# Five small edits to a one-core hybrid decoder layer: turned roots by way of DRAM, block ends shared by VectorE and GpSimd, fill and stores moved

## The chip, the core and the metric

The kernel runs on one core of one Trainium2 chip. The metric is the device time of one execution in microseconds (us). The engines are TensorE (PE, its weight loads PEld), VectorE (DVE), ScalarE (ACT), GpSimd (POOL) and SyncE (SP), which only issues DMAs.

## What is computed

One decoder layer over 1024 tokens of width 1024, in float32. A root-mean-square norm feeds one wide input projection. Mixer A is sparse attention (8 heads in 2 groups, blocks of 128 queries, three branches: compressed, selected, window); mixer B is gated linear attention in chunks. Both are projected up, gated, summed and projected out; a SwiGLU channel mixer and a last norm follow. Cut to what matters:

```python
h = rmsnorm(x, norm_mix)
q_nsa, kv_nsa, g_nsa, q_gla, k_gla, v_gla, lr_gla, r_gla, g_merge = split(h @ w_in)
o_a = nsa_attention(...)            # per 128 queries: gt0 * o_c + gt1 * o_s + gt2 * o_w
o_b = rmsnorm(gla_chunked(...), gla_norm) * silu(r_gla)
merged = gate_a * (o_a @ w_up_nsa) + gate_b * (o_b @ w_up_gla)
x = x + merged @ w_out
h = rmsnorm(x, norm_ffn)
x = x + (silu(h @ w_ffn_gate) * (h @ w_ffn_up)) @ w_ffn_down
return rmsnorm(x, norm_final)
```

## The kernel before, in words

Every large product is made of three TensorE products of split operands: each float32 operand is a high part (rounded by ScalarE, L356, L1150, L1252) and the rest (a subtraction on VectorE or GpSimd, L357, L1151, L1253), and high x high, high x rest and rest x high are summed in PSUM. Activations stand transposed, features on the partitions and tokens along the row, so one matmul is 128x128 weights on 512 tokens.

TensorE's order is written by hand (`manual_schedule` for PE). The order on VectorE, ScalarE, GpSimd and SyncE is made by the tile framework's scheduler, which simulates time, except for instructions in `keep_in_program_order`; the helper `load` (L496) issues a DMA on SyncE in that way.

**Fill.** Work that TensorE can do at any time stands in a queue of small items (`Fill`, L72): a group is three matmuls, planned at 648 ns. `fill.run(ns)` emits groups until their planned time is used up, `flush` emits what is left. So the total of the fill is the same however it is spread.

**First stage (to about 115 us).** The first projection runs as the inputs land; then `work`, a list of groups with other items between them, is flushed in order (L738). `first_roots` (L571) multiplies the sums of squares by ones on TensorE (L573, L574), computes the root `rbc` of each token on ScalarE and VectorE, spread over all partitions, and scales six results. It stands behind 2 of the 16 groups of the first job. `root_turned` (L579) stands behind all 16: eight tiny products with a 1x1 one (L582, 16 instructions, since float32 takes two each) turn row 0 of `rbc` into `rtok`, 128 tokens a column, and VectorE copies it out. `rtok` scales the token-major projections (`token_proj`, L721), first by ScalarE at L756.

**Gated linear attention (about 189 to 300 us).** `gla_stream` (L909) walks 8 chunks: `gla_diag` (L845), seven levels (`gla_level`, L853), and, after level 2, the operands of the next chunk (`gla_prep`, L796: exponents on GpSimd L821 and ScalarE, products `xq` on VectorE L828 and `xx` on GpSimd L832). Each `yield` gives a planned time, and `fill.run(cost * ratio)` puts that share of four projection jobs behind it; `ratio` (L955) is the fill's cost over the sum of the yields. A level writes one of three PSUM banks, which VectorE reads (L861).

**Attention (about 365 to 790 us).** 16 units (two groups of 8 query blocks) of five branches. `Plan` (L109) is a planner with costs and free times of the engines, which decides in what order TensorE gets scores, transposes (L1173, L1157), products with the values (L1182, L1165) and fill. The output of a unit stands in the one PSUM bank `o`; when its last branch is in, `finish` (L1188) empties it: ScalarE copies the lower half of the partitions to the upper (`fo`, L1195), then VectorE adds the two halves in two instructions into `oa` (L1197), and only then may the next unit's first product (L1165) write `o`. The planner knows it as 478 ns of ScalarE followed by 670 ns of VectorE (L214 to L217). `unit` (L1025) prepares the next queries: a load of `rp`, VectorE shuffles, three GpSimd instructions (L1033 to L1035), four DMAs, a ScalarE copy and a GpSimd subtraction (L1044, L1045). Behind the planner's end, `oa` of both groups is split into `oah` and `oal` by ScalarE and VectorE (L1252, L1253), in the middle of what is left of the attention.

**The rest.** Merge and output projection (to about 947 us), then the channel mixer in a form with seven instead of eight block products, 11 pairs of weight blocks up and 11 down. At the end the last products are made in two parts of the tokens, 320 and 192 wide (`finish_half`, L1712): VectorE adds the part to the residual (`plus`, L1588), ScalarE squares (L1593), TensorE sums (L1682), ScalarE and VectorE make the root (L1684 to L1688), and VectorE scales each of eight blocks (`store`, L1602), which SyncE or ScalarE's queue then sends out. `when(i, ...)` puts a step in front of group i.

Of the kernel before, what the change touches and what calls it, by code (L numbers as in the profile page):

```python
# [100 lines left out]
LAT, WAIT, LOADED, COPIED = 155.0, 300.0, 1500.0, 3000.0  # L101
NBIG, NMID, NSMALL = 18, 10, 8
SCRATCH = 2048
FINE, NGATE = 3, 2

UP = (1, 2, 4, 5, 7)

# [1 line left out]
class Plan:  # L109
# [100 lines left out]
    def value(self):  # L210
        _, later, n, b, last = self.pend.popleft()
        later()
        self.t += 218.0 * n if b.br else 436.0
        if last and b.br == 2 and b.j == 1:  # L214
            t = self.on("A", self.t, 478.0)
            t = self.on("D", t, 670.0)
            self.o = t + LAT  # L217

    def run(self):
        ops = dict(T=(self.turn_at, self.turn), S=(self.score_at, self.score), P=(self.value_at, self.value))  # L220
# [21 lines left out]
def layer_kernel(ctx, tc, a, outT):  # L242
# [36 lines left out]
    def ps_o():  # L279
        return bank("o")  # L280
# [30 lines left out]
    def hs(hf):  # L311
        return slice(512 * hf, 512 * (hf + 1))

    def bs(b):
        return slice(128 * b, 128 * (b + 1))
# [255 lines left out]
    def first_roots():  # L571
# [4 lines left out]
        for n in (2, 3, 4, 5, 0, 1):  # L576
            scaled(dst[n], acc[n] if n > 1 else dst[n], n % 2, 0.125 if n < 4 else None)

    def root_turned():  # L579
        ps = ps_o()  # L580
        for b in range(NB):
            PE.matmul(ps[:, b:b + 1], rbc[0:1, bs(b)], ones[0:1, 0:1], start=True, stop=True)  # L582
        V.tensor_copy(rtok, ps[:, :NB])

    def proj(evac, bank=ps_m, fine=False):

# [134 lines left out]
    def token_proj(parts, ncol, evac, after={}):  # L721
        for b in range(NB):
# [6 lines left out]
            for fn in after.get(b, []):  # L729
# [3 lines left out]
    j1, h1, t1, s1 = compress_job(1)  # L733
    lb, wb = token_weights(a["w_b"], 512, 2)
    work = dense([(a["w_t"][3], proj(lambda p, hf: scaled(kg[hf][:, 1, :], p, hf))), j0, key_job(0), j1, key_job(1)], ready=first)
    fill.add(work[:5] + [(900.0, first_roots), (0.0, load_consts)] + work[5:20] + [(400.0, root_turned)] + work[20:48] + h0 + work[48:59] + t0
             + work[59:63] + s0 + work[63:69] + lb[:1] + work[69:74] + lb[1:2] + work[74:84] + h1 + lb[2:] + work[84:])
    fill.flush()  # L738

# [169 lines left out]
    def gla_stream():  # L909
        for c in range(NB):  # L910
            gla_diag(c)
            yield 860
            for i in range(NLV):
                gla_level(c, i)
                yield 430
                if i == 1 and c:
                    gla_out(c - 1)
                    yield 1710
                if i == 1 and c < NB - 1:
                    gla_turn(c)  # L920
                    yield 220
                if i == 2 and c + 1 < NB:
                    gla_prep(c + 1)
                    yield 430
                if i == 3 and c in (1, 3):
                    turn_rank(c // 2 + 2)
                    yield 430
                if i == 4 and c < NB - 1:
                    gla_state(c)
                    yield 860  # L930
                if i == 5 and c in (1, 3):
                    decay(c // 2 + 2)
                    yield 860
        yield 500
        gla_out(NB - 1)
        yield 1710
# [15 lines left out]
        return a["w_t"][8 + 2 * g + j], proj(lambda p, hf: scaled(qr[g][hf][:, j, :], p, hf, 0.125))  # L952

    fill.add(dense([query_job(0, 0), query_job(0, 1)] + [gate_job(j) for j in range(NGATE)]))
    ratio = fill.cost() / (8 * (860 + 7 * 430 + 3220) + 1500)  # L955
    for cost in gla_stream():
        fill.run(cost * ratio)
    fill.flush()
# [89 lines left out]
    class Branch:  # L1048
# [139 lines left out]
        def finish(self):  # L1188
            g, i = self.g, self.i
            po = UN[g, i]["o"]  # L1190
            hf = i // 4
            if oa[g][hf] is None:
                oa[g][hf] = big("oa", shape=(2, 512))
            fo = mid("fo")
            S.activation(fo[0:64, :], po[64:128, :], AF.Copy)  # L1195
            for par in range(2):
                V.tensor_add(oa[g][hf][64 * par:64 * par + 64, :, bs(i % 4)],  # L1197
                             po[0:64, :].rearrange("p (j r q) -> p j r q", j=2, r=2)[:, :, par, :],
                             fo[0:64, :].rearrange("p (j r q) -> p j r q", j=2, r=2)[:, :, par, :])
            del UN[g, i]  # L1200


# [45 lines left out]
    for g in range(NG):  # L1248
        for j in range(2):
            th, tl = big("oah", F32R), big("oal", F32R)  # L1250
            for hf in range(2):
                S.activation(th[:, hs(hf)], oa[g][hf][:, j, :], AF.Copy)  # L1252
                V.tensor_tensor(tl[:, hs(hf)], oa[g][hf][:, j, :], f(th[:, hs(hf)]), OP.subtract)  # L1253
            oah.append(th)
            oal.append(tl)
    fill.flush()
# [339 lines left out]
        else:  # L1596
            sums[n].append(sq)

    def store(blk, mp, hf, c=slice(0, 512)):
        m = mp + (MH if blk[0] == "2" else 0)  # L1600
        xv, at = x1[blk, mp][:, c], slice(512 * hf + c.start, 512 * hf + c.stop)
        V.scalar_tensor_tensor(xv, xv, gains[:, 2, m:m + 1], rbc[:, at], op0=OP.mult, op1=OP.mult)  # L1602
        (S if c.start and mp % 2 else SP).dma_start(outT[:, m, at], xv)


# [85 lines left out]
    ALL = 4  # L1691
# [20 lines left out]
    def finish_half(i, h):  # L1712

        for mp in range(MH):
            when(i + mp // 2, plus, "21", mp, ps["A"][mp], H[h])
            when(i + mp // 2, square, "21", mp, 0, False, H[h])
        when(i + 2, roots, 0, H[h])
        when(i + 2, sums[0].__delitem__, slice(1, None))
        for k in range(2 * MH):
            when(i + 5 + k // 2, store, "12"[k // MH] + "1", k % MH, 0, H[h])  # L1720

    with tc.manual_schedule(engines={mybir.EngineType.SP}):
        for i in range(3):
# [105 lines left out]
```

## Time and profile before

| what | value |
|---|---|
| median of 3 runs | 1596.46 us (1591.89 to 1596.6) |
| the profiled execution, its own time | 1600.53 us |
| its span, first to last instruction | 1598.7 us |
| granted TensorE clock, mean | 0.998 |
| TensorE busy | 1567.5 us, 98% |
| VectorE, ScalarE, GpSimd busy | 1010.4, 814.4, 678.3 us |

The page shares the span out: busy time, forty slices, queues, the chain of work that ended last, the costliest groups. A wait is an engine's idle time before an instruction, with the instruction that ended it. A matmul of 512 columns is shown with 0.39 us, but the next one starts 0.227 us later; stretches of TensorE are therefore read from start to start.

### The profile page before, as it was taken

How to read it: one execution, taken by the hardware profiler on the slowest of the kernel's cores; microseconds unless marked ns; L12 is line 12 of the kernel's file. 1: busy time of each engine (PE TensorE's matmuls, PEld its weight loads, DVE VectorE, ACT ScalarE, POOL GpSimd, SP SyncE). 2: the span in 40 equal slices, each digit the busy share in tenths (PEclk: the TensorE clock that was granted, in tenths of full speed). 3: DMA queues.
4: the chain of work that ended last, by engine and by line, in shares of the span. 5: the costliest groups of instructions: out<-in, count | busy, mean ns of one | idle time of the engine just before them, and what ended most of it. 6: DMA issues, size and time to landing. Idle time of an engine off the chain costs nothing.

```text
span 1598.7 us, 23059 instructions
## 1 busy us (share of the span) xinstructions
PE 1567.5 (98%) x8047; PEld 1311.5 (82%) x8047; DVE 1010.4 (63%) x1653; ACT 814.4 (51%) x1632; POOL 678.3 (42%) x590
## 2 busy tenths in 40 slices
PE   9999999999999999999999999999999999999998
PEld 7888988888888888888877878888888888888887
DVE  7681487586777677677564477744444444499785
ACT  6241555575676676677653344433433444454542
POOL 6110366562212233130144440466666666556570
PEclk9999999999999999999999999999999999999999
DMA  5431112232112122131466532323323323695423
GB/s 182 132 102 61 60 53 68 96 106 83 46 52 65 62 77 65 45 109 60 138 210 206 192 116 73 119 99 106 104 101 105 105 99 99 240 362 162 140 72 125
DMA packets 109590, 179.85 MB, mean 112 GB/s; under 512 B 12689, under 2 KB 29730, under 8 KB 109474
## 3 DMA queue, kind: packets, MB, share of 16 engines
q1 hardware_dynamic: 105442, 171.95, 32.8%
q10 hardware_dynamic: 4032, 6.44, 1.1%
q8 instruction: 63, 1.03, 0.3%
q14 instruction: 53, 0.43, 0.1%
HBM read 128.27 MB, written 45.88 MB: 109 GB/s over the span
## 4 chain that ended last, share of the span: by engine, by line
PE 82%; DVE 6%; DMA 4%; ACT 3%; issue 3%; POOL 2%; SPq 0%; DVEq 0%; POOLq 0%; ACTq 0%
PE m L410 12%; PE d L410 10%; PE m L1397 9%; PE m L1398 9%; PE m L1396 9%; PE m L1759 4%; PE m L1760 4%; PE m L1758 4%; PE o L1182 3%; PE t L1173 3%; PE s L1094 2%; PE s L1095 2%; PE t L725 1%; PE t L726 1%; PE t L727 1%
## 5 line engine op out<-in xcount | busy, mean ns | idle before, releaser
L357 POOL TENSOR_TENSOR wl<-wf,wh 128x512 fp32r<-128x512 f32 x106 | 145.1, 1371 | 323.7 <-ACT wh L356 312.5
L1396 PE MATMUL m<-xt,wh 128*128 128x512 f32 x412 | 160.3, 389 | 0.0
L1397 PE MATMUL m<-xt,wh 128*128 128x512 f32 x412 | 160.3, 389 | 0.0
L1398 PE MATMUL m<-xt,wl 128*128 128x512 f32 x412 | 160.3, 389 | 0.0
L1326 POOL TENSOR_TENSOR wl<-ws,wh 128x512 fp32r<-128x512 f32 x76 | 107.5, 1419 | 73.4 <-ACT wh L1325 73.4
L1151 DVE TENSOR_TENSOR ptl<-t,pth 128x512 fp32r<-128x512 f32 (+1 forms) x168 | 99.4, 596 | 35.5 <-ACT pth L1150 32.5
L1326 POOL TENSOR_TENSOR wl<-wr,wh 128x512 fp32r<-128x512 f32 x69 | 92.2, 1337 | 69.6 <-ACT wh L1325 69.6
L1325 ACT ACTIVATE wh<-ws 128x512 fp32r<-128x512 f32 x76 | 48.0, 632 | 131.4 <-PE m L1397 114.7
L1150 ACT ACTIVATE pth<-t 128x512 fp32r<-128x512 f32 (+1 forms) x168 | 88.0, 525 | 52.8 <-PE t L1173 46.9
L1325 ACT ACTIVATE wh<-wr 128x512 fp32r<-128x512 f32 x87 | 55.0, 632 | 116.9 <-POOL wl L1326 76.4
L1758 PE MATMUL m<-xb,wh 128*128 128x512 f32 x280 | 109.5, 391 | 0.3 <-DVE g L1458 0.3
L1759 PE MATMUL m<-xb,wh 128*128 128x512 f32 x280 | 109.0, 389 | 0.0
L1760 PE MATMUL m<-xb,wl 128*128 128x512 f32 x280 | 108.9, 389 | 0.0
L1326 POOL TENSOR_TENSOR wl<-wd,wh 128x512 fp32r<-128x512 f32 x56 | 82.8, 1482 | 58.3 <-ACT wh L1325 54.7
L410 PE MATMUL m<-hh,wh 128*128 128x512 f32 x240 | 100.4, 419 | 0.0
L1326 DVE TENSOR_TENSOR xb<-ar,xb 128x512 fp32r<-128x512 f32 x73 | 80.3, 1117 | 31.8 <-ACT xb L1325 31.8
L410 PE MATMUL m<-hh,wl 128*128 128x512 f32 x240 | 93.8, 391 | 0.0
L410 PE MATMUL m<-hl,wh 128*128 128x512 f32 x240 | 93.7, 390 | 0.0
L356 ACT ACTIVATE wh<-wf 128x512 fp32r<-128x512 f32 x106 | 65.9, 625 | 53.6 <-PE m L410 25.1
L1396 PEld LDWEIGHTS m<-xt,wh 128*128 128x128 f32 x412 | 77.3, 188 | 16.2
L1398 PEld LDWEIGHTS m<-xt,wl 128*128 128x128 f32 x412 | 77.3, 188 | 16.0
L1397 PEld LDWEIGHTS m<-xt,wh 128*128 128x128 f32 x412 | 77.3, 188 | 16.0
(414 smaller groups left out, 4545.5 us busy)
## 6 DMA issues: line engine op xcount, KB each, us to landing
ar<-actd SPq DMA_DIRECT2D x77, 256.0 KB, 2.8
wf<-in_w_t SPq DMA_DIRECT2D x58, 256.0 KB, 2.9
wr<-in_w_gate SPq DMA_DIRECT2D x44, 256.0 KB, 2.7
wr<-in_w_upf SPq DMA_DIRECT2D x44, 256.0 KB, 2.7
wd<-in_w_down SPq DMA_DIRECT2D x33, 256.0 KB, 5.2
zd<-zt SPq DMA_DIRECT2D x32, 256.0 KB, 2.0
wf<-in_w_out SPq DMA_DIRECT2D x32, 256.0 KB, 3.2
actd<-t SPq DMA_DIRECT2D x30, 256.0 KB, 2.0
```

What stands on the lines that cost most here:

```text
L357: (eng or V).tensor_tensor(wl, wf, f(wh), OP.subtract)
L410: PE.matmul(st["p"], w, x, start=k + i == 0, stop=k == n - 1 and i == 2)
L1150: S.activation(th[:, :c], pt[:, :c], AF.Copy)
L1151: V.tensor_tensor(tl[:, :c], pt[:, :c], f(th[:, :c]), OP.subtract)
L1325: S.activation(th, src, AF.Copy)
L1326: eng.tensor_tensor(tl, src, f(th), OP.subtract)
L1396: PE.matmul(ps, wh[:, c], xh, start=first and k == 0, stop=False, skip_group_check=not first)
L1397: PE.matmul(ps, wh[:, c], xl, start=False, stop=False, skip_group_check=not first)
L1398: PE.matmul(ps, wl[:, c], xh, start=False, stop=k == MH - 1, skip_group_check=not first)
L1758: PE.matmul(dst, wh[:, c], xh, start=first and p == 0, stop=False, skip_group_check=not first)
L1759: PE.matmul(dst, wh[:, c], xl, start=False, stop=False, skip_group_check=not first)
L1760: PE.matmul(dst, wl[:, c], xh, start=False, stop=p == NP - 1, skip_group_check=not first)
```

## The change

Five edits.

1. `root_turned` writes row 0 of `rbc` to DRAM and reads it back with tokens on the partitions, two `load`s on SyncE, in place of eight products and a copy. It needs no place in TensorE's order; its cost in `work` is 0.
2. `first_roots` stands behind 4 groups instead of 2.
3. The yield behind `gla_diag` is 860 + 1200 ns instead of 860, in `ratio` too.
4. `finish`: VectorE copies the upper half out of PSUM (in program order) beside ScalarE's copy, and GpSimd adds; the last unit keeps the old way. The planner counts the longer of 478 (ScalarE) and 550 ns (VectorE). The splits of group 0's `oah` and `oal` go from ScalarE and VectorE to GpSimd.
5. Of the eight blocks of the 320-wide part, the last three are scaled and stored behind the adds of the 192-wide part instead of ahead of them.

```diff
-FINE, NGATE = 3, 2
+FINE, NGATE, AHEAD = 3, 2, 1200
...
         if last and b.br == 2 and b.j == 1:
-            t = self.on("A", self.t, 478.0)
-            t = self.on("D", t, 670.0)
-            self.o = t + LAT
+            self.o = max(self.on("A", self.t, 478.0), self.on("D", self.t, 550.0)) + LAT
...
+    rtd = dr.tile([1, T], F32, name="rtd")
+
     def root_turned():
-        ps = ps_o()
-        for b in range(NB):
-            PE.matmul(ps[:, b:b + 1], rbc[0:1, bs(b)], ones[0:1, 0:1], start=True, stop=True)
-        V.tensor_copy(rtok, ps[:, :NB])
+        load(rtd, rbc[0:1, :])
+        load(rtok, rtd.rearrange("o (b p) -> p (o b)", p=128))
...
-    fill.add(work[:5] + [(900.0, first_roots), (0.0, load_consts)] + work[5:20] + [(400.0, root_turned)] + work[20:48] + h0 + work[48:59] + t0
+    fill.add(work[:7] + [(900.0, first_roots), (0.0, load_consts)] + work[7:20] + [(0.0, root_turned)] + work[20:48] + h0 + work[48:59] + t0
...
             gla_diag(c)
-            yield 860
+            yield 860 + AHEAD
...
-    ratio = fill.cost() / (8 * (860 + 7 * 430 + 3220) + 1500)
+    ratio = fill.cost() / (8 * (860 + AHEAD + 7 * 430 + 3220) + 1500)
...
-            fo = mid("fo")
+            fo, end = mid("fo"), (g, i) == units[-1]
             S.activation(fo[0:64, :], po[64:128, :], AF.Copy)
+            if not end:
+
+                t = mid("fp")
+                tc.keep_in_program_order(V.tensor_copy(t[0:64, :], po[0:64, :]))
+                po = t
             for par in range(2):
-                V.tensor_add(oa[g][hf][64 * par:64 * par + 64, :, bs(i % 4)],
-                             po[0:64, :].rearrange("p (j r q) -> p j r q", j=2, r=2)[:, :, par, :],
-                             fo[0:64, :].rearrange("p (j r q) -> p j r q", j=2, r=2)[:, :, par, :])
+                (V if end else P).tensor_tensor(
+                    oa[g][hf][64 * par:64 * par + 64, :, bs(i % 4)],
+                    po[0:64, :].rearrange("p (j r q) -> p j r q", j=2, r=2)[:, :, par, :],
+                    fo[0:64, :].rearrange("p (j r q) -> p j r q", j=2, r=2)[:, :, par, :], OP.add)
...
             for hf in range(2):
-                S.activation(th[:, hs(hf)], oa[g][hf][:, j, :], AF.Copy)
-                V.tensor_tensor(tl[:, hs(hf)], oa[g][hf][:, j, :], f(th[:, hs(hf)]), OP.subtract)
+                if g:
+                    S.activation(th[:, hs(hf)], oa[g][hf][:, j, :], AF.Copy)
+                else:
+                    P.tensor_copy(th[:, hs(hf)], oa[g][hf][:, j, :])
+                (V if g else P).tensor_tensor(tl[:, hs(hf)], oa[g][hf][:, j, :], f(th[:, hs(hf)]), OP.subtract)
...
-    def store(blk, mp, hf, c=slice(0, 512)):
+    def store(blk, mp, hf, c=slice(0, 512), late=False):
...
-        V.scalar_tensor_tensor(xv, xv, gains[:, 2, m:m + 1], rbc[:, at], op0=OP.mult, op1=OP.mult)
+        ins = V.scalar_tensor_tensor(xv, xv, gains[:, 2, m:m + 1], rbc[:, at], op0=OP.mult, op1=OP.mult)
+        if late:
+            tc.keep_in_program_order(ins)
...
         for k in range(2 * MH):
-            when(i + 5 + k // 2, store, "12"[k // MH] + "1", k % MH, 0, H[h])
+
+            late = h == 0 and k > MH
+            when(i + (NP - ALL + 2 if late else 5 + k // 2), store, "12"[k // MH] + "1", k % MH, 0, H[h], late)
```

## Rows read from the trace of the kernel before

**Rows 1.** The page, busy time (us), share and instructions of each engine.
```profile
PE 1567.5 (98%) x8047; PEld 1311.5 (82%) x8047; DVE 1010.4 (63%) x1653; ACT 814.4 (51%) x1632; POOL 678.3 (42%) x590
```

**Rows 2.** TensorE's waits, 185 to 300 us: total, times, longest (us).
```profile
PE t L859 <- DVE xq L828: 2.3, 4, 0.8
PE t L859 <- DVE at L861: 2.1, 2, 1.6
```

**Rows 3.** TensorE's waits, 365 to 790 us.
```profile
PE t L1173 <- DVE rr L1105: 1.9, 1, 1.9
PE o L1165 <- DVE oa L1197: 1.7, 2, 1.2
PE s L1071 <- ACT p L1125: 1.7, 1, 1.7
PE t L1173 <- DVE ptl L1151: 1.3, 2, 0.7
```

**Rows 4.** Timeline of TensorE, first stage: start us, us, instruction, idle before.
```profile
38.25 0.39 PE L410 MATMUL m<-hh,wh 128*128 128x512 f32 x1
...
39.38 0.39 PE L410 MATMUL m<-hh,wl 128*128 128x512 f32 x1
40.89 0.49 PE L573 MATMUL o<-ssh,onesr 128*128 128x512 f32 x1 [1.12 <-ACT ssh L568]
41.62 0.50 PE L574 MATMUL o<-ssl,onesr 128*128 128x512 f32 x1 [0.23 <-DVE ssl L569]
...
42.55 0.39 PE L410 MATMUL m<-hh,wh 128*128 128x512 f32 x1
...
52.19 1.94 PE L582 MATMUL o<-ones,rbc 1*128 1x1 f32 x16
54.06 0.50 PE L410 MATMUL m<-hh,wh 128*128 128x512 f32 x1
```

**Rows 5.** DMA issues: tiles, queue, count, KB each, median us to landing.
```profile
zd<-zt SPq DMA_DIRECT2D x32, 256.0 KB, 2.0
...
w<-in_cmp_w SPq DMA_DIRECT2D x2, 64.0 KB, 7.1
...
ggain<-in_gla_norm SPq DMA_DIRECT2D x1, 0.5 KB, 3.2
```

**Rows 6.** Timeline of SyncE's queue and of ScalarE, first stage.
```profile
51.54 2.90 SPq L355 DMA_DIRECT2D wf<-in_w_t  x2
...
120.60 0.69 ACT L756 ACTIVATE vt<-t,rtok 128x512 f32<-128x512 f32 x1 [0.60 <-PE t L727]
```

**Rows 7.** Timeline of ScalarE and VectorE, the end of one attention unit.
```profile
754.20 0.59 ACT L1195 ACTIVATE fo<-o 64x512 f32<-64x512 f32 x1
...
754.83 0.85 DVE L1197 TENSOR_TENSOR oa<-o,fo 64x256 f32<-64x256 f32 x2 [0.76 <-ACT fo L1195]
```

**Rows 8.** Lines L1033 and L1110, attention: ns min/median/max, first to last start.
```profile
L1033 POOL TENSOR_TENSOR qa<-qr,rp x15: 728/738/751, 374.1 to 709.0; 128x256 f32<-128x256 f32 x15
...
L1110 DVE TENSOR_TENSOR rr<-rr,gz x64: 138/159/1147, 380.5 to 770.3; 128x1 f32<-128x1 f32 x64
```

**Rows 9.** Window of short units: PE, PEld, DVE, ACT, POOL busy, clock, DMA.
```profile
545.00:600.00 55.00, 52.63 (x340) 45.79 (x339) 39.41 (x127) 39.89 (x144) 19.41 (x20) 0.97 0.22 66
```

**Rows 10.** Timeline of VectorE and GpSimd, 733 to 737 us.
```profile
733.10 1.27 POOL L357 TENSOR_TENSOR wl<-wf,wh 128x512 fp32r<-128x512 f32 x1 [1.19 <-ACT wh L356]
...
733.46 1.46 DVE L1253 TENSOR_TENSOR oal<-oa,oah 128x512 fp32r<-128x512 f32 x1
...
736.18 0.41 DVE L1151 TENSOR_TENSOR ptl<-t,pth 128x256 fp32r<-128x256 f32 x1
```

**Rows 11.** Timeline of VectorE and TensorE, the last 15 us.
```profile
1585.15 3.79 DVE L1602 SCALAR_TENSOR_TENSOR x<-x,gains,rbc 128x320 f32<-128x320 f32 x8
...
1589.65 1.57 PE L1682 MATMUL m<-sq,minus 128*128 128x192 f32 x8 [0.16 <-ACT sq L1593]
...
1592.50 0.36 DVE L1687 SCALAR_TENSOR_TENSOR nv<-m,nv 128x192 f32<-128x192 f32 x1 [2.50 <-ACT nv L1686]
```

## The prediction

> **What bounds the kernel now.** I read the page first: TensorE is busy for 1567.5 of 1598.7 us [rows 1]. So 31 us is all that its visible idle time holds, and the change can gain only where TensorE waits, or where it does work that can go elsewhere. The next view is therefore TensorE's waits, stretch by stretch: in the gated linear attention two lines hold 4.4 us, all on VectorE [rows 2]; in the attention four lines hold 6.6 us [rows 3]. The third view is the timeline of TensorE around the roots [rows 4]. There the cadence is to be seen first: five matmuls from 38.25 to 39.38 us, so 0.227 us each, whatever their shown length. Against it a hole: four root products and the way to the next group take 3.17 us, from 39.38 to 42.55, where five places of the cadence are 1.13. The waits in it are for the split sums of squares. Later, sixteen tiny products hold TensorE from 52.19 to 54.06. Last, the timeline of the end, where VectorE's chain alone sets the time [rows 11].
>
> **The change part by part.**
>
> *Turned roots by DRAM.* Sixteen instructions go from TensorE, which waits for nothing there: 54.06 - 52.19 = **1.87 us** on the path [rows 4]. The VectorE copy that goes with them is off the path. Added are two DMAs on SyncE, the second waiting for the first to land. The trace has no DMA of 1024 four-byte pieces. The nearest are a 256 KB store that lands in 2.0 us, a load of 128 four-byte pieces in 3.2 us and, farthest, a 64 KB load behind big ones in 7.1 us [rows 5]. I take 2.0 + 3.2 = 5.2 us, with 2 x 7.1 = 14.2 as the upper end. `rbc` is whole before the tiny products read it at 52.19, so `rtok` stands at about 57.4, or 66.4 at worst. Its first reader starts at 120.60 [rows 6], so its lateness costs nothing. What can cost is the queue: SyncE stands still for the landing of the first DMA. Behind it are the weight loads issued at 51.54 [rows 6] and, because `load` keeps its order, the small inputs of the next compression job. Those weights belong to a later job: weights are asked for up to three tiles ahead. I take 0; if TensorE comes to wait, the price is one landing beyond the cover, at most 1 us. Nothing below zero: the work on TensorE is simply gone.
>
> *Roots two groups on.* Six matmuls move in front of the roots: 6 x 0.227 = **1.36 us** of the hole is filled [rows 4]. The second root product still waits for the rest of the squares until 41.62, so the roots are not later: the first can start at 39.38 + 7 x 0.227 = 40.97 against 40.89 before. The bounds are 0 and 1.36; what the roots release starts when it did, so I take the upper end.
>
> *Fill in front of the first level.* The fill is four jobs of 16 groups at 648 ns, 41,472 ns, and the yields sum to 58,220 ns, with the change 67,820: `ratio` falls from 0.712 to 0.611. Behind `gla_diag` the fill grows from 860 x 0.712 = 612 to 2060 x 0.611 = 1260 ns, one group more. Between the preparation of the next chunk and its `gla_diag` the yields of 3010 ns shrink from 2143 to 1841. So the time from the preparation to the first level grows by 0.35 us net a chunk. The waits of rows 2 are six, 4.4 us in all; 0.35 off each is 2.1, and later levels lose a seventh of their fill. I take **1.5 us**. Bounds: all 4.4 gone on one side, a loss of 1 us (half the longest wait at a bank, 1.6 us) on the other.
>
> *Unit ends.* Before, the bank is free after 0.59 of ScalarE and then 0.85 of VectorE: 754.20 to 755.68, 1.48 us [rows 7]. After, the two copies run side by side. The VectorE copy has no row; the two sums of rows 7 together go over the same 512 columns, so it lies between one of them (0.42) and both (0.85), and I take 0.75. The bank is free some 0.7 us sooner. Two waits on it are 1.7 us together, the longer one 1.2 [rows 3]: the shorter goes, 0.5, and 0.7 of the longer. I take **1.2 us**, between a loss of 1 (the new planner's order may make such a wait elsewhere) and 1.7. The planner's own account of the bank falls from 155 + 478 + 155 + 670 + 155 = 1613 to 155 + 550 + 155 = 860 ns, so the order of everything behind the first unit can shift.
>
> GpSimd gets two sums for 15 units. The nearest row is a 128x256 sum at 0.74 us [rows 8], so 30 x 0.74 = 22 us. Where units are short it is busy for 19.4 of 55 us [rows 9], so there is room. But VectorE can be held up: its one-column product takes 159 ns in the median and 1147 at most [rows 8], and a subtraction that begins inside a GpSimd instruction takes 1.46 us [rows 10]. I charge **-0.4 us**, a fiftieth of the 22 us, with 0 and -2 as ends.
>
> The Trainium skill has a rule for this (page "SBUF — State Buffer", section "Who interferes with whom"): a VectorE instruction with two SBUF inputs and a GpSimd instruction that reads SBUF exclude one another, and whichever starts second waits for the whole of the first. The trace agrees for a few of the 64 products (1147 against 159 ns). If every added sum met such a product, VectorE would lose the whole 22 us, and the gain of this part would be a loss.
>
> *Splits of group 0 on GpSimd.* At 733.46 VectorE puts 1.46 us of `oal` ahead of a maximum, and a second `oal` ahead of the rest `ptl` at 736.18 [rows 10]. TensorE's longest attention wait, 1.9 us, falls right behind [rows 3]. Without the two subtractions about 2 us leave that queue. I take **1.5 us** of the 1.9; ends: all of it, and a loss of 0.5 if GpSimd's four copies and four subtractions (between 0.74 and 1.29 us each by rows 8 and 10) hold weights back. Their cover is GpSimd's idle time, two thirds of it even among the short units [rows 9].
>
> *Last stores.* Eight scalings take 3.79 us, 0.47 each, until 1588.94; three of them, 1.42 us, leave VectorE's way before the last adds, and fit into its wait of 2.50 us for the root [rows 11]. Their DMAs still go out on SyncE ahead of the last eight. But the last products themselves end shortly before the sums at 1589.65, which waited only 0.16 us for the squares. I take **0.3 us**, between 0 and 1.4.
>
> **Sum:** 1.87 + 1.36 + 1.5 + 1.2 - 0.4 + 1.5 + 0.3 = 7.3 us. The sum is made against the profiled execution, 1600.53 us by its own clock, which becomes 1593.2. That execution lies 4.1 us above the median of the runs shown, 1596.46; taken off the median, the forecast is **1589.1 us**.
>
> **Rivals.**
>
> *The waits move, they don't go.* The fill is the same in total and the planner draws a new order, so the attention and the linear attention give back what they gain. For it: the waits of rows 2 and 3 are many and short, each ended by an engine that is itself behind. Against it: the bank and the `oal` waits have causes that the change takes away. Left are 1.87 + 1.36 + 0.3 = 3.5 us: 1592.9 us.
>
> *More goes than is counted.* The wait of 1.7 us on ScalarE's `p` [rows 3] lies among the short units, where the granted clock is 0.97 over 55 us [rows 9]: with the lower of its levels, half, that is 3.3 us at 1.2 GHz, 1.65 us lost. If the new order has neither, 3.35 us more go: 1585.7 us.
>
> *GpSimd's sums stand in the way.* At each of 15 unit ends VectorE's small products, from which the probabilities are scaled, begin behind a sum and wait for it; TensorE then waits for the transposes' input. The two sums of an end are 1.48 us. The gain without this charge is 7.7 us, so it is eaten at 0.5 us an end. The change is slower by a measurable amount at 0.84. At 1.0 us an end it costs 15: 1596.5 - 7.7 + 15 = 1603.8 us. For it speaks the longest product of rows 8; against it that the median one is not held at all with GpSimd a third busy. The page named above states this exclusion; how often it strikes is what rows alone tell.
>
> **How the numbers follow.** About 0.3% (4.8 us) is what a measurement of this kernel can tell from no change: the borders are 1591.7 and 1601.2. The forecast has 0.60, with its own range from 1586 to 1592.5 by the ends of the fill and of the unit ends; about a tenth of it is above the border. The moved waits have 0.21, mostly within 0.3%; the greater gain 0.12; the sums in the way 0.07, two thirds of it measurably slower. Faster: 0.54 + 0.12 + 0.03 = 0.69; slower 0.05; the rest, 0.26, the same. The range takes in the greater gain and the moved waits with the ends of the small terms: 1583.5 to 1596 us; outside are the third rival and the tails.
>
> **What would show it.** No L582, and TensorE's next job some 3.2 us sooner; one small gap or none at L573; `rtok`'s reader not waiting for a DMA. In the linear attention, fewer waits on `xq` ahead of a first level. No wait of L1165 on VectorE or ScalarE above 0.5 us; none at 730 to 740 us behind `oal`. In the tail, three 320-wide scalings between the last adds and the root. The prediction is wrong if TensorE's waits between 365 and 790 us sum to 7 us or more, if the one-column products grow in number beyond 500 ns and TensorE waits behind them, or if weight loads behind the two DMAs come late.

## The result and the profile after

| | before | after |
|---|---|---|
| median, us | 1596.53 (6 runs, 1591.89 to 1600.96) | 1587.95 (6 runs, 1585.85 to 1590.14) |
| ratio of the times | | 0.9947, 95% interval 0.9928 to 0.9966 |
| the profiled execution, its span | 1600.53, 1598.7 | 1586.64, 1584.8 |

The change is faster by 8.6 us. The two profiled executions differ by 13.9 us: the one of before lies 4.0 us above its median, the one of after 1.3 below. So the traces are compared stage by stage, and with further traces of the same kernels.

The page of the kernel after, busy time, answers to [rows 1]: TensorE is 5.2 us less busy, GpSimd 29 us more.

```profile
PE 1562.3 (99%) x8031; PEld 1310.9 (83%) x8031; DVE 1006.9 (64%) x1633; ACT 811.9 (51%) x1628; POOL 707.4 (45%) x628
```

TensorE's waits over the whole span (total, times, longest) answer to [rows 2, 3]; L857, L871, L1163, L1171 are the L859, L873, L1165, L1173 of before, and L636 is the L638. The first line is of before, the others of after; "issue" means that the view names no instruction that ended the wait.

```profile
PE m L638 <- issue: 0.7, 2, 0.6
```
```profile
PE m L636 <- issue: 3.0, 2, 2.4
...
PE t L857 <- DVE xq L826: 1.6, 2, 0.8
PE s L1092 <- ACT p L1123: 1.6, 1, 1.6
...
PE t L1171 <- DVE ptl L1149: 1.3, 3, 0.6
PE t L857 <- DVE vs L748: 0.9, 1, 0.9
...
PE o L1163 <- DVE fp L1197: 0.3, 1, 0.3
...
PE d L871 <- DVE at L859: 0.3, 1, 0.3
```

The waits for `rr` (1.9) and for a bank behind `at` (2.1, now 0.3) are as good as gone, those for `xq` and for the bank `o` have shrunk. At the top stands a grown one at L636, the first products of the compression job's hidden layer ("hidden products"), at 70 us and so outside the stretches of [rows 2, 3]. The reader of `rtok`, in [rows 6] at 120.60, waits for TensorE as before and for no DMA:

```profile
121.11 0.69 ACT L754 ACTIVATE vt<-t,rtok 128x512 f32<-128x512 f32 x1 [0.60 <-PE t L725]
```

**Where that wait comes from.** Four names are needed. `pe` is a small table that the compression job loads, `w` its weights; `pb` is a sum of 16 products of the two, which VectorE makes as a chain of 16 steps; `kst` and `krt` are scalings on VectorE that empty PSUM banks behind the projections. First TensorE around the roots (timeline of after), beside [rows 4]: no hole, the root products at 40.91 stand behind their neighbours.

```profile
40.68 0.40 PE L408 MATMUL m<-hh,wl 128*128 128x512 f32 x1
40.91 0.40 PE L571 MATMUL o<-ssh,onesr 128*128 128x512 f32 x1
41.18 0.50 PE L572 MATMUL o<-ssl,onesr 128*128 128x512 f32 x1
...
42.12 0.40 PE L408 MATMUL m<-hh,wh 128*128 128x512 f32 x1
```

Then SyncE's queue. In the kernel before, the constants and the compression job's inputs (`w`, `pe`) are issued behind three weight loads, and the fourth weight load comes behind `pe`, at 51.54 [rows 6], though the queue issues nothing from 42.3 on. SyncE's own waits end there on GpSimd's split `wl` of an earlier weight, so the load waits for a free buffer:

```profile
35.64 3.81 SPq L355 DMA_DIRECT2D wf<-in_w_t  x3
...
41.87 0.44 SPq L497 DMA_DIRECT2D pe<-in_cmp_pe  x1
```

In the kernel after, the fourth weight load (issued at 49.91, the end of the first row) and `rtd`, which waits for the roots, stand in front of them:

```profile
35.20 15.03 SPq L353 DMA_DIRECT2D wf<-in_w_t  x4
50.46 0.24 SPq L495 DMA_DIRECT2D rtd<-rbc  x1
...
52.31 0.38 SPq L495 DMA_DIRECT2D rtok<-rtd  x1
...
54.31 0.43 SPq L495 DMA_DIRECT2D pe<-in_cmp_pe  x1
```

VectorE waits for `pe`, and the scaling `krt` that empties the bank stands in its queue behind the 15 further steps of the chain `pb` (timelines of VectorE and TensorE, after); `krt` ends at 70.23, and the hidden products start at 70.34. In all fourteen traces they start 0.10 or 0.11 us behind the end of `krt`. The two rows of TensorE are of after; the row behind them is the `krt` of before, where VectorE stood ready and waited for TensorE:

```profile
67.49 0.40 PE L408 MATMUL m<-hh,wl 128*128 128x512 f32 x1
70.34 5.83 PE L636 MATMUL m<-w,kst 128*63 128x128 f32 x36 [2.45 <-issue]
```
```profile
70.71 0.69 DVE L544 TENSOR_TENSOR krt<-m,rbc 128x512 f32<-128x512 f32 x1 [2.82 <-PE m L410]
```

VectorE's rows of after:

```profile
61.07 0.29 DVE L625 TENSOR_SCALAR pb<-w,pe 128x128 f32<-128x128 f32 x1 [3.72 <-DMA pe<-in_cmp_pe]
61.39 3.98 DVE L627 SCALAR_TENSOR_TENSOR pb<-w,pe,pb 128x128 f32<-128x128 f32 x8
65.40 1.41 DVE L615 TENSOR_TENSOR kst<-m,rbc 64x512 f32<-64x512 f32 x2
66.84 2.68 DVE L627 SCALAR_TENSOR_TENSOR pb<-w,pe,pb 128x128 f32<-128x128 f32 x7
69.54 0.69 DVE L542 TENSOR_TENSOR krt<-m,rbc 128x512 f32<-128x512 f32 x1
```

TensorE had finished the projection's products 3.5 us sooner than before (the last starts at 67.49 instead of 70.97), lost 2.45 in that wait, and then ran at half clock. The windows of after show it (PE, PEld, DVE, ACT, POOL busy, then the granted clock, DMA share, GB/s). The granted clock is 0.50 from 71 to 74 us, the lower of the two levels (1.2 GHz): 0.12 + 3 x 0.5 + 0.09 of a microsecond's clock is lost, 1.7 us.

```profile
70.00:71.00 1.00, 0.66 (x5) 0.69 (x6) 0.88 (x3) 0.00 (x0) 0.00 (x0) 0.88 0.73 264
71.00:72.00 1.00, 1.00 (x7) 1.00 (x6) 0.97 (x3) 0.00 (x0) 0.00 (x0) 0.50 0.27 95
72.00:73.00 1.00, 1.00 (x6) 1.00 (x5) 0.96 (x2) 0.00 (x0) 0.00 (x0) 0.50 0.06 17
73.00:74.00 1.00, 1.00 (x7) 1.00 (x6) 0.30 (x2) 0.78 (x2) 0.00 (x0) 0.50 0.00 0
74.00:75.00 1.00, 1.00 (x10) 1.00 (x9) 0.97 (x2) 0.48 (x1) 0.00 (x0) 0.91 0.00 0
```

**The stages.** Lengths in us, from the start of one TensorE instruction to another's, in all traces of this study. *Front*: first root product to the first product of the token projection; *linear*: first to last product of the linear attention; *attention*: first score to last value product; *merge*: first merged product to the first product of the output projection; *output*: from there to its last; *tail*: last channel product to the end. A star marks a stage with a stretch of half clock.

| kernel | front | linear | attention | merge | output | tail |
|---|---|---|---|---|---|---|
| before | 74.07 | 109.82 | 408.62* | 59.99 | 95.69 | 9.51 |
| same_again (before) | 75.69* | 109.76 | 407.10 | 59.70 | 93.85 | 9.53 |
| only_dram | 72.03 | 109.76 | 406.26 | 58.15 | 92.09 | 9.54 |
| only_roots | 74.27* | 109.81 | 408.59* | 59.93 | 93.92 | 9.53 |
| only_ahead | 74.09 | 106.58 | 408.03* | 59.85 | 93.24 | 9.52 |
| only_ends | 74.11 | 109.79 | 404.55 | 61.16* | 91.33 | 9.51 |
| only_splits | 74.12 | 109.74 | 405.20 | 59.87 | 90.41 | 9.52 |
| after | 74.56* | 106.57 | 403.23 | 58.23 | 91.70 | 9.55 |
| after_again (after) | 72.68 | 106.58 | 405.77* | 58.22 | 92.28 | 9.55 |
| late_turn | 74.17* | 106.56 | 402.57 | 58.32 | 93.73 | 9.55 |
| turn_on_pe | 72.79 | 106.58 | 403.58 | 59.05 | 94.01 | 9.52 |
| early_loads | 76.58* | 106.59 | 404.93* | 58.86 | 92.51 | 9.55 |
| pe_early | 75.87* | 106.58 | 404.43 | 60.87* | 91.15 | 9.56 |
| pe_and_ident | 70.73 | 106.62 | 403.64 | 59.10 | 93.42 | 9.55 |

The output stage goes from 90.4 to 95.7 with no order by edit (before itself has 95.69 and 93.85): most of what the first two profiles differ by beyond the medians lies there. There TensorE waits for split weights (`wl`) 4.1 us in before, 1.2 in after. That is no gain of the change.

### The profile page after: what moved, and what is told of

Read it like the earlier page. It is cut to its first block, busy times and chain, and to the rows that moved or that the text cites. A ratio compares the mean times of both kernels' runs of the same rounds, so it can differ in the third digit from the quotient of the medians.

```text
span 1584.8 us, 23061 instructions
## 1 busy us (share of the span) xinstructions
PE 1562.3 (99%) x8031; PEld 1310.9 (83%) x8031; DVE 1006.9 (64%) x1633; ACT 811.9 (51%) x1628; POOL 707.4 (45%) x628
## 4 chain that ended last, share of the span: by engine, by line
PE 86%; DVE 5%; DMA 3%; ACT 2%; issue 2%; POOL 1%; SPq 0%; DVEq 0%; ACTq 0%; POOLq 0%
PE m L408 12%; PE d L408 10%; PE m L1404 9%; PE m L1405 9%; PE m L1403 9%; PE m L1769 4%; PE m L1770 4%; PE m L1771 4%; PE o L1180 3%; PE t L1171 3%; PE s L1092 2%; PE s L1093 2%; PE t L723 1%; PE t L725 1%; PE t L724 1%
```

## Experiments

Ratios are to the kernel before on the same chip. Five of the experiments put one edit, or one part of edit 4, alone into the kernel before; edit 5 was not run alone.

**late_turn.** Changed kernel, the two DMAs of the turned roots ten places later in `work`.

```diff
- work[7:20] + [(0.0, root_turned)] + work[20:48]
+ work[7:30] + [(0.0, root_turned)] + work[30:48]
```

> The changed kernel with one thing moved: the two DMAs of the turned roots are emitted ten items later, behind the loads of the first compression job. Queue theory: in the changed kernel SyncE waits for the root in front of those loads, so the small input pe lands at 61 us instead of 47.5, VectorE's sums pb come late, the copy that frees a bank comes late, and TensorE waits 2.4 us at the first product of the compression (L636) and then runs 3.4 us at half clock. With the loads in front: pe lands before 50 us, the wait at L636 falls below 0.5 us, the clock stays whole there, and the token projection starts at 111 to 112 us instead of 115.5; the kernel is 3 to 4.5 us faster than the changed one, near 1584 us. Rival (TensorE only reaches the compression earlier than VectorE can be ready, whatever carries the turned roots): the wait at L636 stays above 1.5 us, and the time stays within 1 us of the changed kernel's.

1587.95 us, ratio 0.9941 (0.9927 to 0.9955). `pe` was issued at 54.47 all the same, and TensorE waited 2.08 us at L636. So the queue theory in this form falls: the DMAs of the roots are not alone in the way; the fourth weight load and the constants still are.

**turn_on_pe.** Changed kernel with edit 1 undone: the 16 tiny products and the copy of the kernel before.

> The changed kernel with the turned roots back on TensorE. Queue theory: 1.9 us more work on TensorE, but no wait at L636 and no half clock behind it (4.3 us), so the token projection starts at 113 to 114 us instead of 115.5 and the kernel is about 2 us faster than the changed one, near 1586 us: the DRAM way costs more than it saves as it stands. Rival: the wait at L636 stays, and the kernel is 1.9 us slower than the changed one, near 1590 us.

1590.92 us, ratio 0.996 (0.9946 to 0.9974). Without `rtd` and `rtok` in the queue `pe` was issued only 1.1 us sooner (53.17), `krt` ended at 70.79, and the wait at L636 was 0.98 us: TensorE came 2.0 us later than in the changed kernel (69.52 against 67.49) and so waited less.

**only_dram.** The kernel before with edit 1 alone.

> The kernel before with the turned roots by way of DRAM and nothing else. Queue theory: pe lands at 60 us or later, TensorE waits 1 us or more at L636, and the token projection starts no earlier than 114 us against 115.0 before; the time is within 2 us of the kernel before. Rival (the wait comes from the roots' place): no wait at L636 above 0.5 us, the token projection starts at 113.1 us, and the kernel is 1.9 us faster.

1591.52 us, ratio 0.997 (0.9959 to 0.9981). The front is 2.04 us shorter, where 1.87 was the forecast. Yet `pe` is late here too (issued at 54.28, behind `rtd`); `krt` ends at 69.23, which is 0.44 after the last product starts, and nobody waits. The lateness is hidden as long as TensorE is no earlier than this. The whole gains more than the front: 4.8 us by the ratio (3.0 to 6.5). This trace has some 1.7 us less in the merge and no half clock; where the rest comes from is not shown.

**same_again.** The kernel before, unchanged, one more trace.

> The kernel before, unchanged, profiled once more. It tells how much of the difference of the two profiles (13.9 us, where the medians differ by 8.6) is run to run, and in which stage. Theory: the step in the merge and the output projection (first product on merged halves to last: 95.7 us before, 91.7 after; and 60.0 against 58.2 us ahead of it) is spread between executions, so this profile shows one of 93 us or less for the same program in that stage, and first and attention stages within 1 us of the first profile. Rival: that stage takes 95 to 96 us again, so one of the edits shortened it.

1598.52 us. Half clock came at another place, right behind the tiny products of L582, and not in the attention (windows, columns as above):

```profile
54.00:57.00 3.00, 3.00 (x13) 2.44 (x13) 2.74 (x10) 0.00 (x0) 0.21 (x1) 0.78 0.54 130
57.00:60.00 3.00, 3.00 (x10) 2.36 (x9) 0.00 (x0) 0.00 (x0) 0.00 (x0) 0.65 0.38 135
```

**only_roots.** The kernel before with edit 2 alone.

> The kernel before with the second edit alone (the first roots and the constants two groups of the projection later); the roots are still turned by TensorE. The forecast's term: TensorE finds its roots' operands ready, the 1.36 us wait at the first roots goes, and everything after is 1.36 us sooner (token projection at 113.6). Theory A now (SP's order): the fourth weight load now stands in front of the constants, w1, w2 and pe on SP, pe is issued after 50 and lands at 58 to 60 instead of 47.5, and TensorE waits about 1 us for it at the first hidden products, so the token projection starts at 114.0 to 114.7 and the kernel gains 0.3 to 1 us, the rest of the time within 0.1%. If pe lands by 50 and a wait comes there nevertheless, theory A falls.

1596.26 us, ratio 0.9993 (0.9982 to 1.0003). The wait of 1.1 us at the first roots is gone, `pe` is issued at 54.88, VectorE waits 2.5 us for it. The front is 74.27, with half clock behind L582 in it; at full clock that would be some 72.6, 1.5 less than before. The expected wait at the hidden products did not come in this execution: TensorE itself was 1.7 us late. The median is 1.7 us under that of before, within the interval of no change.

**early_loads.** Changed kernel with `load_consts` and the compression job's four loads ahead of the roots.

```diff
- work[:7] + [(900.0, first_roots), (0.0, load_consts)] + work[7:20]
+ work[:5] + [(0.0, load_consts), (0.0, early[0])] + work[5:7] + [(900.0, first_roots)] + work[7:20]
```

> The changed kernel, with the constants and the first compress job's own loads (both halves of w1, w2, pe) issued ahead of the fourth weight load and of the two DMAs that turn the roots, as the kernel before had them. Theory A (what the change lost in its front was lost in SP's order: pe was issued at 54.31 us and landed at 60.97, because the fourth weight load, which waits until 49.9 for a free buffer, was put in front of it): pe is issued near 42 and lands near 48, the 2.4 us wait of TensorE at L636 and the 3.41 us of half clock right behind it (1.7 us of loss) go, and the token projection starts at 111.4 instead of 115.47, 3.6 us before the kernel before, which is nearly the 3.23 us forecast for the two edits together; the kernel is some 4 us faster than the changed one, near 1584. Theory B (the wait is set by the roots themselves coming two groups later, with VectorE's and ScalarE's work behind them): pe lands at 48 but TensorE still waits 1 us or more at the first hidden products, the half clock comes all the same, the token projection starts at 114.5 or later and the time is within 1 us of the changed kernel's.

1590.33 us, ratio 0.9953 (0.9939 to 0.9967): no gain over the changed kernel. `pe` was issued at 42.00 and the wait at L636 is gone, but the scheduler put four casts of constants and two steps of `pb`, with waits of 0.94 us for a constant and 0.57 us for `pe`, between the links of the roots' chain on VectorE. The scaling `kg` came late, and TensorE waited 3.04 us for it at 51, with half clock from 53.0 on. Theory A had named the load and missed the queue behind it.

**after_again.** The changed kernel, beside these on one chip.

> The changed kernel as it is, on the same chip as the runs beside it, for a direct comparison. Both theories: 1588 us, ratio to the kernel before 0.995. In its trace the wait of TensorE at L636 is again 2.0 to 2.5 us with pe landing near 61 and half clock behind it; the token projection starts near 115.3. The merge of the branches and the output stage may differ from the first trace by 2 us either way.

1589.7 us, ratio 0.9947 (0.9934 to 0.996). The wait at L636 is there (2.18 us), half clock behind it is not: the granted clock stays 1.00 from 69 to 75 us. The front is 72.68.

**pe_early.** As early_loads, but only the four loads are moved and the chain `pb` keeps its place on VectorE.

```diff
+ work[:5] + [(0.0, early[0])] + work[5:7] + [(900.0, first_roots), (0.0, load_consts)] + work[7:20]
...
- V.tensor_scalar(b, d["w1"][0][:, 0, :], d["pe"][:, 0:1], None, op0=OP.mult)
+ tc.keep_in_program_order(V.tensor_scalar(b, d["w1"][0][:, 0, :], d["pe"][:, 0:1], None, op0=OP.mult))
```

> The changed kernel with the first compress job's four loads (w1 twice, w2, pe) alone issued ahead of the weight load that waits for a buffer; the constants stay where the change put them, and the chain of sums that needs pe keeps its place on VectorE behind the scalings of the first projection. Theory C (VectorE's order is what counts: with pe late its chain of 16 products stands still for 3.7 us and holds up kst and krt, which is the wait at L636; with pe early and the chain let forward, as in the run with the loads and constants early, the scalings come late and TensorE waits 3.0 us at its next projection instead): here neither wait is there, VectorE's wait for pe of 3.7 us is gone, the last scaling of the next job (krt, ended at 69.5) is there by 67, the first hidden products follow with under 0.3 us of wait, the token projection starts at 110.8 to 111.6 without half clock (113.23 in the changed kernel's second trace, 115.47 in its first), and the kernel is 2 to 3 us faster than the changed one, ratio to before 0.993. Theory B (the roots two groups later hold up VectorE's whole front, whatever pe does): a wait of over 1 us remains somewhere before 75 us and the time is that of the changed kernel within 1 us.

1590.32 us, ratio 0.9941 (0.9922 to 0.9959). The wait of 3.0 us was there again, with another late load in front: `ident`, now issued behind `pe`, and its cast in the middle of the roots' chain (timelines of VectorE and TensorE, pe_early):

```profile
46.38 0.23 DVE L338 CAST identb<-ident 128x128 bf16<-128x128 f32 x1 [2.77 <-DMA ident<-in_consts]
```
```profile
54.01 0.50 PE L408 MATMUL m<-hh,wh 128*128 128x512 f32 x1 [3.04 <-DVE kg L542]
```

**pe_and_ident.** As pe_early, with the five small constants and the cast of `ident` issued ahead of `pe`, as the changed kernel has them.

```diff
+ work[:5] + [(0.0, small_consts), (0.0, early[0])] + work[5:7] + [(900.0, first_roots), (0.0, load_consts)] + work[7:20]
```

> The changed kernel with the first compress job's four loads ahead of the fourth weight load, as in the run before, and the five small constants (ident, tri, cmul, ggain, w2b) and the cast of ident issued ahead of them, where the changed kernel has them; the two large constants stay behind the roots. In the run before ident was issued behind pe (41.4 us), landed at 46.4, and VectorE's cast of it stood in the middle of the roots' chain, which held it for 2.77 us: TensorE's wait of 3.0 us at 51 was that. Theory C (the front's waits are made by VectorE standing in line behind a late load, first pe, then ident): VectorE's order is that of the changed kernel and no load is late, so the scalings of the first job end at 53.6 as there, the chain for pe is through by 66, there is no wait of TensorE over 0.3 us at 50 to 56 and at the first hidden products, the token projection starts at 110.8 to 111.6 (2 us before the changed kernel's 113.23), and the time is 2 us under the changed kernel's, 1586 to 1588, ratio 0.9925 to 0.994. Theory B (VectorE's own work is too much for this front): a wait of over 1 us stays before 75 us and the token projection starts after 112.5.

1587.15 us, ratio 0.9935 (0.992 to 0.9949). VectorE no longer waits for a load, `krt` is early, and TensorE has 0.15 us at the hidden products (timelines of VectorE and TensorE, pe_and_ident):

```profile
57.88 0.29 DVE L635 TENSOR_SCALAR pb<-w,pe 128x128 f32<-128x128 f32 x1
...
67.32 0.69 DVE L544 TENSOR_TENSOR krt<-m,rbc 128x512 f32<-128x512 f32 x1 [0.88 <-PE m L410]
```
```profile
67.57 0.39 PE L410 MATMUL m<-hh,wl 128*128 128x512 f32 x1
68.11 5.16 PE L646 MATMUL m<-w,kst 128*63 128x128 f32 x45 [0.15 <-issue]
```

The front is 70.73, 3.34 under before (the forecast of the two edits was 3.23) and 1.95 under the changed kernel without half clock. The projection itself began at 112.14, behind the expected 111.6, as the roots began at 41.41 (40.55 there) and a second job's hidden products waited 1.1 us instead of 0.6. Theory C holds for the mechanism; of the time, the median of the best version is below both kernels', but its interval overlaps that of the change.

**only_ahead.** The kernel before with edit 3 alone.

> The kernel before with the third edit alone (1200 more of fill in front of a chunk's first level). The forecast's term was 1.5 us with bounds of -1 and 4.4. The three traces of changed kernels all show the gated-attention stage (token projection's start to the last of its products) 3.25 us shorter, and those without this edit 0.07: if this edit alone makes it, the stage is 3.2 us shorter here, TensorE's waits for xq ahead of the first levels fall from some 3 us to under 2 us, and the time falls by 3.2 us, to 1593.3 (ratio 0.998). The rival is that part of it comes from the roots turned by DMA or from the other order of the loads in front: then 1 to 2 us here, 1594.5 to 1595.5.

1594.18 us, ratio 0.9975 (0.9964 to 0.9986). The linear stage is 3.24 us shorter, as in every trace with this edit. Its waits are, to the digit, those of the changed kernel (1.6, 0.9, 0.3):

```profile
PE t L859 <- DVE xq L828: 1.6, 2, 0.8
PE t L859 <- DVE vs L750: 0.9, 1, 0.9
PE d L873 <- DVE at L861: 0.3, 1, 0.3
```

**only_ends.** The kernel before with the unit ends of edit 4 (copy, sums on GpSimd, the planner's cost).

> The kernel before with the fourth edit's first part alone: at a unit's end VectorE copies, GpSimd adds twice, and the planner's cost goes with it; the splits stay on ScalarE and VectorE. If the two waits at L1165 behind the sums (0.73 and 1.43 us lost at 639 and 656) are all that it takes away, the attention stage is 1.6 us shorter (2.16 to 0.53 us lost there), and the wait of 1.9 us behind rr at 737 stays. If the planner's other order is what moves the waits, that one goes as well and the stage is 3.4 us shorter, as in the changed kernel (403.2 to 405.8 us against 406.3 to 408.6 before). Time: 1.6 us faster (ratio 0.999), or 3.4 (0.9979).

1597.2 us, ratio 0.9995 (0.9982 to 1.0007). In its trace the attention is 404.55; the five traces without this part or the splits, half clock taken off at 1.7, have 406.3 to 407.1, mean 406.7. So 2.1 us in this one trace (those five alone spread over 0.8); the medians differ by 1.5, and the interval of the ratio holds 1. The wait for the bank falls from 1.7 to 0.3, and the one for `rr` stays whole:

```profile
PE t L1171 <- DVE rr L1103: 1.9, 1, 1.9
PE s L1092 <- ACT p L1123: 1.3, 1, 1.3
PE t L1171 <- DVE ptl L1149: 1.3, 3, 0.6
PE o L1163 <- DVE fp L1197: 0.3, 1, 0.3
```

**only_splits.** The kernel before with the splits of group 0 on GpSimd.

> The kernel before with the fourth edit's second part alone: the splits of the first group's sums on GpSimd instead of ScalarE and VectorE. If VectorE's splits are what rr stands behind at 734 to 737, TensorE's wait for rr (1.9 us, 2.0 us lost) goes and the attention stage is 1.9 us shorter; the two waits at L1165 stay as they were (1.7 us). If not, the wait stays or turns into one for p or ptl of a like size, and the stage is within 0.5 us. Time: 1.9 us faster (ratio 0.9988), or the same.

1594.92 us, ratio 0.9976 (0.9964 to 0.9988). The wait for `rr` is gone, the bank's is as before; the attention is 405.20, 1.5 us under that mean:

```profile
PE o L1165 <- DVE oa L1197: 1.7, 2, 1.2
PE t L1173 <- DVE ptl L1151: 1.4, 2, 0.8
PE s L1071 <- ACT p L1125: 1.4, 1, 1.4
```

## Why the prediction was right, and where its terms were not

The forecast was 1589.1 us, the median is 1587.95, and "faster" came. The sum, 7.3 us, met 8.6; its parts met less well, and that the total is so near is partly luck: the front gave 1.8 us less than was counted (1.9 less again where half clock came), while the fill gave 1.7, the attention 0.9 and the merge over 1 us more.

- **Turned roots, 1.87, and roots two groups on, 1.36.** Each price is right: 2.04 alone, and 3.34 together once no load is late (pe_and_ident). In the change itself only 1.4 us came without half clock (74.07 to 72.68), and 0.5 were lost with it (74.56). The step that failed is "what can cost is the queue ... I take 0 ... at most 1 us". It named the right queue and the right inputs, but looked at the two DMAs only. Moving the roots also let the fourth weight load pass in front of those inputs, and what waited was not TensorE for a weight but VectorE for `pe`, with `krt` in line behind a chain of 16 steps. The price was 1.9 to 2.3 us at L636 (beyond the 0.15 that stands there in every trace) and, in two of the three traces of after, after_again and late_turn, 1.7 of half clock. So "what the roots release starts when it did" failed as well.
- **Fill, 1.5.** Mis-sized: 3.24, inside its bounds. The list of waits accounts for 4.7 - 2.8 = 1.9 of it: the wait behind `at` fell from 2.1 to 0.3, where the step had taken 0.35 us off each wait alike. That list misses the rest because it counts a wait from the modelled end of the matmul before. Read from start to start, over the plain cadence of each kind of matmul, the places with a listed wait lost 5.9 us in before and 3.5 in only_ahead, 2.4 less. The remaining 0.8 went in pieces of under 0.3 us at places with no listed wait; beside it, TensorE's fill comes in 50 runs instead of 58.
- **Unit ends, 1.2, GpSimd's lock, -0.4, splits, 1.5.** Together 2.3 forecast; in the attention 403.5 (mean of the seven traces with both, half clock taken off) against 406.7 is 3.2. Splits 1.5 as priced, ends 2.1, each from one trace, where traces of the same attention spread over 0.8 (five without these parts) and 1.9 us (the seven with both). The prices of the parts can be read off the changed kernel's tiles (ns min/median/max): the copy 682, for which 750 was taken; GpSimd's sum 730, for which 740 was taken; and the one-column product unchanged beside [rows 8].

```profile
L1197 DVE COPY fp<-o x15: 671/682/683, 415.9 to 746.5; 64x512 f32<-64x512 f32 x15
...
L1200 POOL TENSOR_TENSOR oa<-fp,fo x30: 720/730/932, 416.6 to 748.1; 64x256 f32<-64x256 f32 x30
...
L1108 DVE TENSOR_TENSOR rr<-rr,gz x64: 140/159/1146, 377.8 to 761.5; 128x1 f32<-128x1 f32 x64
```

  For these products the charge for the lock was 0. The exclusion that the Trainium skill states (page "SBUF — State Buffer", section "Who interferes with whom") strikes rarely here: 22.5 us of added sums on GpSimd left the 64 products at 13.3 us in all, against 13.4 before, and four of them over 500 ns, against five. Elsewhere VectorE was held a little: two scalings of `p`, 128x128, that overlapped a sum in after (at 557.42 and 568.97) took 0.84 us where the shortest take 0.33. Over all VectorE instructions of the attention, the time above the shortest of the same form, where it is over 0.1 us, adds up to 10.1 to 12.1 us in the eight traces with the sums and 8.6 to 11.4 in the six without. So VectorE paid between nothing and some 2 us, and TensorE shows no new wait for it. The third rival, "GpSimd's sums stand in the way", falls.
- **Last stores, 0.3.** Right up to the issue, nothing at the end. The timeline of VectorE in the tail of after shows three scalings between the last adds and the root; beside [rows 11] the wait for the root is 0.93 instead of 2.50.

```profile
1571.17 2.40 DVE L1609 SCALAR_TENSOR_TENSOR x<-x,gains,rbc 128x320 f32<-128x320 f32 x5
1574.55 1.36 DVE L1595 TENSOR_TENSOR x<-x,m 128x192 f32<-128x192 f32 x4 [0.98 <-PE m L1771]
1575.82 1.47 DVE L1609 SCALAR_TENSOR_TENSOR x<-x,gains,rbc 128x320 f32<-128x320 f32 x3
1578.23 0.36 DVE L1696 SCALAR_TENSOR_TENSOR nv<-m,nv 128x192 f32<-128x192 f32 x1 [0.93 <-ACT nv L1695]
```

  Counted from the start of the last channel product (1589.22 before, 1575.24 after), the root's first step on VectorE comes 2.99 us behind it instead of 3.28, 0.3 sooner; the end of the span 9.55 behind it instead of 9.51, and likewise in the seven traces with this edit (9.52 to 9.56) and the seven without (9.51 to 9.54). The 0.3 is still there when the last store that the trace shows has landed (8.17 instead of 8.45 in these two traces). It is given back in the closing steps of the program: GpSimd's last semaphore instruction, which all engines wait for, comes 0.35 to 0.37 us behind the one before it in the seven traces with this edit, and 0.06 in the seven without. Why was not tried; those seven kernels are also the only ones with both parts of edit 4 on GpSimd.
- **Not forecast.** The merge is 58.2 to 59.1 in the changed kernels and 59.7 to 60.0 in five traces with at most one edit; in before TensorE waits 1.4 us there for `wh` (L356). But only_dram has 58.15 and no such wait, with the same order on TensorE and the same order of issue on SyncE. What moves it stays open.

Of the rivals, the moved waits came true in one stage, the front, and in none of the others: the waits between 365 and 790 us sum to 3.4 us, under the 7 that would have made the forecast wrong. The greater gain did not come: the wait for `p` stayed at 1.6 us in after and 1.8 in after_again, there with half clock behind it. Of the signs of a wrong forecast the last came true in part: `w` and `pe` behind the two DMAs were 12 us late, while the next weight load was issued at 54.78 instead of 54.11 and TensorE waited for none.

By stages the change has 1.4 (front at full clock) + 3.2 + 3.2 + 0 = 7.8 us and 1.2 to 1.6 in the merge; the medians say 8.6. The single edits can't be added up to it. By their ratios they gained 4.8 (only_dram), 1.1 (only_roots), 4.0 (only_ahead), 0.8 (only_ends) and 3.8 us (only_splits), 14.5 together without edit 5, where the whole gained 8.5. Each of these figures has an interval of some 2 to 3 us either way, so most of the difference of 6 could be noise. The front explains a part: there edits 1 and 2 are worth 2.0 and 1.5 alone and 1.4 together.

## What to carry to other kernels

When a step moves, list the order of the issuing queue before and after: a load that waits for a buffer, let pass in front of small inputs, made them 12 us late, and an engine that stands for one of them holds up everything in line behind it. One late input may be hidden alone and show only when another edit makes the consumer earlier, so price edits of one stage together. And take a second trace of the unchanged kernel before explaining a difference of two single traces: here 5 of the 14 us were not the change's.

## What the runs showed of the hardware

Half clock comes by the execution, not by the program alone. Thirteen stretches were seen ahead of the tail in fourteen traces, the one shown above 3.4 us long and worth 1.7 (one, in early_loads, was twice as long). Each begins in or right behind a place where TensorE had stood or had run tiny products: the waits at 579 us, L636, `rr`, `kg`, L582, two waits of 0.6 to 1.0 us close together in the merge. Waits of 0.9 to 3.0 us had it behind them; so had the tiny products, during which TensorE counts as busy. The same place goes without it in another trace of the same kernel (L636 in after and after_again, L582 in before and same_again). So a removed wait is worth its length and, in some executions, 1.7 us more; a single trace can't show how often.
